# A hybrid decoder step on one core: order of the side work, order of the last head pair, and the memory of the trunk's tiles

## The chip, the cores and the metric

The kernel runs on one core of one Trainium2 chip. The metric is the device time of one launch in microseconds (us); smaller is better. Every number of a profile comes from one profiled execution; the time before is the median of three runs.

## The reference, cut to what matters

One layer of a decoder with 1024 features is computed in float32 for a prompt of 2048 tokens and for 8 sample requests of 4 tokens each (32 sample tokens), which share the weights:

```
a = rmsnorm(h); [qa|fa|ia|ga|qb|kb|vb] = a @ w_in          # 7 groups of 512 columns
h = h + concat(HGRN2(qa,fa,ia,ga), DilatedAttn(qb,kb,vb)) @ w_o
h = h + ConvFFN(rmsnorm(h))                                 # 1024 -> 2816 -> 1024, gate with a 3-tap convolution
h = h + sigmoid(rmsnorm(h) @ w_ple_gate) * (p @ w_ple_proj)
y = rmsnorm(h)
```

HGRN2 is a gated linear recurrence of 4 heads of 128. DilatedAttn has 8 heads of 64; each query reads keys of three dilations (window 128 step 1, window 512 step 4, window 2048 step 16), each dilation has its own softmax statistics, and the three are combined by their maxima and sums. A sample request reads a cache of 2048 keys and values beside its new tokens and a stored recurrent state. Outputs are y for both, the recurrent states, the caches and the convolution's last rows.

## The kernel before, in words

Matmuls that need float32 precision are done as three fast ones: every operand is split into a rounded high part and a low part (on ACT, L913 or L982, and on DVE, L914 or L983), and `mm3` (L136 to L138) adds high x high, high x low and low x high in PSUM.

Four stages follow each other. The input stage multiplies by `w_in` in two token blocks; the recurrence of the prompt (`hgrn_unit`, 8 units) runs beside its second block. Then come the prompt's attention and the sample requests side by side. The last is the trunk: output projection, FFN and embedding, each over three token blocks of 704, 704 and 672 tokens (`TRUNK`, the last with the 32 sample tokens), in the order out 0, 1, 2, FFN 0, 1, 2, embedding 0, 1, 2.

`attn_phase` treats the 8 heads as four pairs p. Per pair there are two kinds of blocks (di = 0: the step-4 residue classes, di = 1: the near window) in four query chunks c of 512 tokens; a unit is one block of 128 queries for both heads, or for one head where a block has over two tiles of keys. This makes 40 units per pair, 160 in all, in the order of the list `units`. A loop over x makes the scores of unit x (L719, L720, then minimum on DVE, L724, and exponential on ACT, L725), transposes the probabilities of unit x - 2 (L732, copied at L734) and multiplies those of unit x - 3 with the values (L744). Keys and queries of a pair lie in four large tiles (qS, q4, kH, kL); the next pair's are loaded into `stage` tiles and laid there during the present pair's last units. When both kinds of a chunk are done, `merge` combines them: statistics go through DRAM (`stats_d`, L650), coefficients too (`coef_d`, L672 and L676, `cf`), POOL multiplies (L681), DVE adds (L683), and the result is stored in row 4 + p of `mix_d` (L684). A merge is spread over the turns 0, 2, 3, 4, 8 and 9 after its last unit.

Beside it runs a generator `others`: the last unit of the prompt's recurrence, the sample's recurrence (`hgrn_sample`), and the sample's attention (`attn_sample`). The last reads 32 tiles `skt` of 1 MB of the cache, adds a mask (`sneg`), takes the exponential, multiplies by how many dilations contain a key (`smult`, L860; `smultn`, L861), transposes (L870), multiplies with the values (L884, L889), and stores into `mix_d` (L897). The loop that drives both makes one turn of the attention, and on two of each five turns one step of `others`, with high priority:

```
    for turn in itertools.count(1):
        if not step(main, 1):
            break
        if turn % 5 in (1, 3):
            first(side, 1)
```

The order on each engine's queue is not the order of the program. A planner simulates the time line, takes instructions by priority (the program's order) as their inputs come ready in its simulation, and gives tiles a place among the free ones of their pool. Each engine then executes its list in order. A pool that is opened with `reuse_waits="tile"` (the helper `pools`) passes its memory on tile by tile; the pools `hsp`, `s_c`, `s_k` and `s_w` of the sample work are opened without it. Pools are laid one after the other from one end of SBUF, those of the recurrence from the other end.

In the trunk, `wide` takes a tile of 704 floats per partition from the pool `tw` (48 of them): raw activations, their high and low parts, residuals h, and working tiles of the FFN. Weights come through `raw` (pool `tr`, 8 tiles), are split into `w` (pool `tp`, 9 tiles of 4 KB), and accumulate in 8 PSUM banks (`tm`). `out_prep` loads the 8 rows of `mix_d` of a block and splits them; `out_block` first multiplies two output tiles m together, row after row (`dense_first`), then the other six. While a block's last products run, the next block's preparation is advanced (`ahead`). `ffn_prep` makes sums and differences of the halves of its 8 rows (L1084 to L1087, split at L982, L983), because the FFN's gate and up products use Strassen's seven products (`strassen`); it holds 28 tiles for the whole FFN block, beside h.

## Time and profile before

| | |
|---|---|
| median of 3 runs | 3115.41 us (3111.81 to 3116.32) |
| profiled execution | 3108.7 us, span 3106.7 us |
| mean granted TensorE clock | 0.980 |
| busy share PE / PEld / DVE / ACT / POOL | 96 / 90 / 72 / 42 / 26% |
| DMA | 468.54 MB, mean 151 GB/s |

PE is TensorE's matmuls, PEld its weight loads, DVE VectorE, ACT ScalarE, POOL GpSimd, SP the queue that issues nearly all loads and stores. The span runs from the first to the last instruction. The granted clock is a share of 2.4 GHz; 0.50 is the lower level, 1.2 GHz. A window's row gives the stretch, its length, the busy time of each engine with the number of instructions, the clock, the busy share of the DMA engines (a figure may round above 1) and GB/s.

### The profile page before, as it was taken

What the parts mean: (1) busy time and instruction counts of PE and PEld (TensorE: products, weight loads), DVE (VectorE), ACT (ScalarE), POOL (GpSimd) and SP (SyncE); (2) the same over time, 40 slices, a digit from 0 to 9 for tenths busy, and PEclk for the clock granted to TensorE, in tenths of its full rate; (3) what the DMA queues carried; (4) which work ended last, traced back from release to release, by engine and by line L of the source; (5) the groups of instructions that cost most, each with busy time, mean ns of one, the idle gap of its engine ahead of it and who ended that gap; (6) DMA issues with size and microseconds to landing.
All of it is one profiled execution on the core that took longest, in us unless ns stands there. A gap on an engine that the chain in (4) does not pass through costs nothing.

```text
span 3106.7 us, 52031 instructions
## 1 busy us (share of the span) xinstructions
PE 2995.4 (96%) x19035; PEld 2781.7 (90%) x19035; DVE 2240.2 (72%) x4670; ACT 1296.8 (42%) x2813; POOL 808.2 (26%) x655
## 2 busy tenths in 40 slices
PE   9999999999889996999999999999999999999998
PEld 8988899987667654998999998999998999999997
DVE  7424667857688874469777779777778877787786
ACT  4111422222366654335444445444444444445443
POOL 1211122222344431003222223322222322232331
PEclk9999999999999997999999999999999999999998
DMA  6334333342536898675434443434433544436453
GB/s 186 98 114 137 105 103 110 103 150 71 152 85 164 251 275 253 212 254 189 163 114 138 136 131 137 167 134 143 137 115 128 185 144 144 137 111 210 141 176 130
DMA packets 265505, 468.54 MB, mean 151 GB/s; under 512 B 39520, under 2 KB 107232, under 8 KB 263456
## 3 DMA queue, kind: packets, MB, share of 16 engines
q1 hardware_dynamic: 261664, 398.22, 40.4%
q10 hardware_dynamic: 3584, 66.98, 6.1%
q8 instruction: 150, 2.46, 0.3%
q14 instruction: 107, 0.88, 0.1%
HBM read 381.60 MB, written 150.48 MB: 171 GB/s over the span
## 4 chain that ended last, share of the span: by engine, by line
PE 52%; DVE 5%; issue 1%; ACT 1%; DMA 1%; SPq 0%; DVEq 0%; ACTq 0%
PE mm L136 17%; PE mm L137 17%; PE mm L138 17%; DVE w L914 1%; DVE w L1171 1%; DVE w L983 0%; PE mm L123 0%; ACT w L982 0%; DVE w L1256 0%; DMA w<-in_pT_dram 0%; DVE w L1084 0%; DVE w L1245 0%; PE mm L108 0%; DMA w<-hn_d 0%; DVE w L1287 0%
## 5 line engine op out<-in xcount | busy, mean ns | idle before, releaser
L137 PE MATMUL mm<-w 128*128 128x352 f32 (+3 forms) x3768 | 1211.2, 322 | 3.2 <-DVE w L983 1.9
L136 PE MATMUL mm<-w 128*128 128x352 f32 (+3 forms) x3768 | 1176.5, 323 | 30.7 <-ACT w L982 10.4
L138 PE MATMUL mm<-w 128*128 128x352 f32 (+3 forms) x3768 | 1204.0, 322 | 0.0
L136 PEld LDWEIGHTS mm<-w 128*128 128x128 f32 x3768 | 705.7, 189 | 38.4 <-ACT w L982 22.0
L137 PEld LDWEIGHTS mm<-w 128*128 128x128 f32 x3768 | 714.3, 190 | 6.8 <-DVE w L983 4.6
L138 PEld LDWEIGHTS mm<-w 128*128 128x128 f32 x3768 | 712.4, 189 | 0.1
L914 DVE TENSOR_TENSOR w<-raw,w 128x512 fp32r<-128x512 f32 x718 | 556.7, 791 | 161.3 <-ACT w L913 155.4
L913 ACT CAST w<-raw 128x512 fp32r<-128x512 f32 x718 | 430.9, 619 | 380.5 <-PE mm L138 251.0
L1171 DVE TENSOR_TENSOR w<-w,mm 128x352 f32<-128x352 f32 (+1 forms) x528 | 257.2, 506 | 89.8 <-PE mm L138 79.9
L1103 POOL TENSOR_TENSOR raw<-raw 128x512 f32<-128x512 f32 x66 | 99.7, 1511 | 739.1 <-DMA raw<-in_w_down_dram 203.4
L1111 POOL TENSOR_TENSOR raw<-raw 128x512 f32<-128x512 f32 x66 | 94.6, 1433 | 398.5 <-DVE w L914 398.5
L725 ACT ACTIVATE P<-P,st 128x256 f32<-128x256 f32 (+3 forms) x256 | 134.6, 528 | 85.2 <-DVE st L724 82.9
L1126 ACT COPY s<-mm 128x352 f32<-128x352 f32 (+1 forms) x198 | 88.1, 445 | 173.4 <-PE mm L138 167.2
L301 PE MATMUL mm<-wh,xh 128*128 128x512 f32 x352 | 142.0, 405 | 0.0
L303 PE MATMUL mm<-wh,xl 128*128 128x512 f32 x352 | 140.9, 401 | 0.0
L302 PE MATMUL mm<-wl,xh 128*128 128x512 f32 x352 | 140.5, 400 | 0.0
L142 POOL TENSOR_SCALAR wh<-wraw 128x512 fp32r<-128x512 f32 x96 | 73.0, 771 | 244.7 <-PE o L137 83.0
L136 PE MATMUL mm<-xh,wh 128*128 128x384 f32 (+2 forms) x384 | 125.1, 330 | 5.8 <-ACT xh L199 5.2
L724 DVE CUSTOM_DVE_ANT_0 P<-S,mask 128x256 f32<-128x256 f32 (+3 forms) x256 | 105.9, 445 | 29.3 <-PE S L720 22.8
L964 POOL TENSOR_TENSOR w<-w 128x704 f32<-128x704 f32 (+2 forms) x42 | 76.3, 1823 | 192.7 <-ACT w L963 191.9
L138 PE MATMUL mm<-xh,wl 128*128 128x384 f32 (+2 forms) x384 | 125.0, 329 | 1.2 <-DVE wl L224 1.2
L224 DVE TENSOR_TENSOR wl<-wraw,wh 128x512 fp32r<-128x512 f32 x104 | 83.0, 817 | 59.0 <-POOL wh L142 53.8
(330 smaller groups left out, 5046.7 us busy)
## 6 DMA issues: line engine op xcount, KB each, us to landing
raw<-in_w_gate_dram SPq DMA_DIRECT2D x132, 256.0 KB
raw<-in_w_up_dram SPq DMA_DIRECT2D x132, 256.0 KB
raw<-in_w_down_dram SPq DMA_DIRECT2D x132, 256.0 KB
out_sk_dram<-in_cache_k_dram ACTq DMA_DIRECT2D x56, 584.0 KB
out_sv_dram<-in_cache_v_dram ACTq DMA_DIRECT2D x56, 584.0 KB
wraw<-in_w_in_dram SPq DMA_DIRECT2D x104, 256.0 KB
w<-h_d SPq DMA_DIRECT2D x48, 352.0 KB
raw<-in_w_ple_gate_dram SPq DMA_DIRECT2D x64, 256.0 KB
```

The lines of the kernel that those rows point to most:

```text
L136: PE.matmul(ps, lhsT=wh, rhs=xh, start=first, stop=False, skip_group_check=read)
L137: PE.matmul(ps, lhsT=wh, rhs=xl, start=False, stop=False, skip_group_check=read)
L138: PE.matmul(ps, lhsT=wl, rhs=xh, start=False, stop=last, skip_group_check=read)
L301: PE.matmul(ps, lhsT=xh[k][:, js], rhs=wh, start=k == 0, stop=False)
L302: PE.matmul(ps, lhsT=xh[k][:, js], rhs=wl, start=False, stop=False)
L303: PE.matmul(ps, lhsT=xl[k][:, js], rhs=wh, start=False, stop=k == NK - 1)
L724: V.tensor_tensor_reduce(pe, s[:, w * i:w * i + w], bl.mask, 1.0, 3e38, ALU.add, ALU.min, mn)
L725: A.activation(pe, pe, AF.Exp, bias=mn, scale=-1.0, accum_out=st[:, bl.r, hh, 0:1])
L913: A.copy(w[:, 0], raw)
L914: V.tensor_sub(w[:, 1], raw, f32(w[:, 0]))
L1103: G.tensor_add(s1, a21, a22)
L1171: V.tensor_add(h[m][:, cs], h[m][:, cs], ps[:, :H])
```

## The change

The side work: the sample's attention runs before the sample's recurrence, both in pools with `reuse_waits="tile"`; `s_k` has three tiles instead of two; a side step follows every second turn. The tables `smult` and `smultn` and their two multiplications are gone: the logarithm of the multiplicity stands in `sneg` and `snegn`, which are added before the exponential. The attention: units of pair 3 are in the order chunk by chunk, both kinds of a chunk after each other; the last addition of its merges is on POOL; `v` has 6 buffers instead of 5, `P` 4 instead of 5. The trunk: its pools are laid in another order, `tw` has 40 tiles, and a new pool `thh` has 8 of the same size (`held`), used for the raw rows in `out_prep`, for h in the FFN and for the high parts in embedding block 1; out block 0 starts with one output tile instead of two.

```diff
@@ -632,7 +632,7 @@
 
         def values_chunk(p, di, c):
 
-            raw = wk.tile([128, 4, 128], F32, name="v", bufs=5)
+            raw = wk.tile([128, 4, 128], F32, name="v", bufs=6)
             cols = v_d[512 * c:512 * c + 512, 128 * p:128 * p + 128]
             if di == 0:
                 SP.dma_start(raw, cols.rearrange("(i r) c -> i r c", r=4))
@@ -680,7 +680,7 @@
             for i in range(2):
                 G.tensor_mul(parts[i], parts[i], cf[:, i])
             yield
-            V.tensor_add(parts[1], parts[1], parts[0])
+            (G if p == 3 else V).tensor_add(parts[1], parts[1], parts[0])
             SP.dma_start(mix_d[:, 4 + p, 512 * c:512 * c + 512], parts[1])
 
         class Block:
@@ -714,7 +714,7 @@
                 bl.st = st
                 w = 128 * bl.nk
                 s = pS.tile([128, 512], F32, name="S")
-                self.pe = wk.tile([128, 512], F32, name="P", bufs=5)
+                self.pe = wk.tile([128, 512], F32, name="P", bufs=4)
                 for i, hh in enumerate(self.heads):
                     PE.matmul(s[:, w * i:w * i + w], lhsT=bl.q(hh), rhs=bl.k(kH, hh), start=True, stop=False)
                     PE.matmul(s[:, w * i:w * i + w], lhsT=bl.q(hh), rhs=bl.k(kL, hh), start=False, stop=True)
@@ -746,12 +746,14 @@
 
         units, begin = [], {}
         for p in range(4):
-            for di in range(2):
-                for c in range(4):
-                    begin[p, di, c] = len(units)
-                    for r in range(4):
-                        bl = Block(p, di, c, r)
-                        units += [Unit(bl, (0, 1))] if bl.nk < 3 else [Unit(bl, (0,)), Unit(bl, (1,))]
+
+            order = [(di, c) for di in range(2) for c in range(4)] if p < 3 else \
+                [(di, c) for c in range(4) for di in range(2)]
+            for di, c in order:
+                begin[p, di, c] = len(units)
+                for r in range(4):
+                    bl = Block(p, di, c, r)
+                    units += [Unit(bl, (0, 1))] if bl.nk < 3 else [Unit(bl, (0,)), Unit(bl, (1,))]
         n = len(units)
         todo, staged = {}, []
 
@@ -812,12 +814,8 @@
 
     def attn_sample(cp, kp, wk, pps):
         NKEY = 1024 + NS
-        mult = cp.tile([128, 1024], F32, name="smult")
-        SP.dma_start(mult, I["s_mult"])
         neg = cp.tile([128, 1024], F32, name="sneg")
         SP.dma_start(neg, I["s_neg"])
-        multn = cp.tile([128, 2, NS], F32, name="smultn")
-        SP.dma_start(multn, I["s_multn"])
         negn = cp.tile([128, 2, NS], F32, name="snegn")
         SP.dma_start(negn, I["s_negn"])
         hmask = cp.tile([128, 512], F32, name="shm")
@@ -857,8 +855,6 @@
             V.tensor_tensor(nm[:, 0:1], nm[:, 0:1], nm[:, 1:2], op=ALU.min)
             V.tensor_tensor(nm[:, 0:1], nm[:, 0:1], nm[:, 2:3], op=ALU.min)
             A.activation(P, P, AF.Exp, bias=nm[:, 0:1], scale=-1.0)
-            V.tensor_mul(P[:, :1024], P[:, :1024], mult)
-            V.tensor_mul(P[:, 1024:], P[:, 1024:], multn[:, g])
             V.reduce_sum(l[:, 0:1], P, axis=mybir.AxisListType.X)
             V.reciprocal(l[:, 1:2], l[:, 0:1])
             yield
@@ -899,7 +895,7 @@
 
 
 
-    def trunk(cst, rp, ev, sm, tw, sh, wp, pmm):
+    def trunk(cst, rp, ev, sm, tw, hp, sh, wp, pmm):
         def raw_tile():
             return rp.tile([128, 512], F32, name="raw")
 
@@ -926,6 +922,9 @@
 
         def wide(T, dt=F32):
             return tw.tile([128, 704], dt, name="w")[:, :T]
+
+        def held(T, dt=F32):
+            return hp.tile([128, 704], dt, name="h")[:, :T]
 
         def dense(parts, xh, xl, ks=range(NK), ends=(0, NK - 1)):
 
@@ -996,7 +995,7 @@
             s.order = (2, 3, 4, 5, 0, 1, 6, 7) if b == 0 else range(NK)
             s.mh, s.ml = {}, {}
             for k in s.order:
-                raw = wide(T)
+                raw = held(T)
                 SP.dma_start(raw, mix_d[:, k, t0:t0 + T])
                 s.mh[k], s.ml[k] = halves(raw, T)
                 yield
@@ -1005,7 +1004,8 @@
             t0, T, _ = TRUNK[b]
             H = T // 2
             chunks = ((0, H), (H, H))
-            first = dense_first([weight(I["w_o"][m]) for m in range(2)], chunks, s.mh, s.ml, s.order)
+            n1 = 2 if b else 1
+            first = dense_first([weight(I["w_o"][m]) for m in range(n1)], chunks, s.mh, s.ml, s.order)
             flush(1)
             ssq = wide(T)
             h = []
@@ -1019,10 +1019,10 @@
             more()
             more()
             for m in range(NK):
-                w = None if m < 2 else weight(I["w_o"][m])
+                w = None if m < n1 else weight(I["w_o"][m])
                 more()
                 hm = h[m]
-                for ps, c0, cn in dense_all(w, chunks, s.mh, s.ml, first[m] if m < 2 else None):
+                for ps, c0, cn in dense_all(w, chunks, s.mh, s.ml, first[m] if m < n1 else None):
                     V.tensor_add(hm[:, c0:c0 + cn], ps[:, :cn], hm[:, c0:c0 + cn])
                 SP.dma_start(h_d[:, m, t0:t0 + T], hm)
                 sum_sq(m, hm, ssq, T)
@@ -1259,7 +1259,7 @@
                     V.tensor_sub(lo, gms[i], f32(hi))
                     parts[i] = hi, lo
                 if f == 0:
-                    h = [wide(T) for _ in range(NK)]
+                    h = [held(T) for _ in range(NK)]
                     for m in range(NK):
                         SP.dma_start(h[m], h_d[:, m, t0:t0 + T])
                 todo.extend(downs(b, f, parts, h))
@@ -1280,7 +1280,7 @@
             s.ssq = wide(T)
             for m in range(NK):
                 hm = raw[m]
-                hi, lo = wide(T, F32R), wide(T, F32R)
+                hi, lo = (held if b == 1 else wide)(T, F32R), wide(T, F32R)
                 g = gains[:, 2, m:m + 1]
                 A.activation(hi, hm, AF.Copy, scale=g)
                 sum_sq(m, hm, s.ssq, T, eng=G)
@@ -1470,17 +1470,17 @@
         for h in range(4):
             SP.dma_start(O["ps"][h], S[h])
         hgrn_st.close()
-        with tc.tile_pool(name="hsp", bufs=1) as hp:
-            yield from hgrn_sample(hp, pps)
-        with tc.tile_pool(name="s_c", bufs=1) as cp, tc.tile_pool(name="s_k", bufs=2) as kp, \
-                tc.tile_pool(name="s_w", bufs=1) as wk:
-            yield from attn_sample(cp, kp, wk, pps)
+        with ExitStack() as st:
+            pool = pools(st)
+            yield from attn_sample(pool("s_c", 1), pool("s_k", 3), pool("s_w", 1), pps)
+        with ExitStack() as st:
+            yield from hgrn_sample(pools(st)("hsp", 1), pps)
 
     side = others()
     for turn in itertools.count(1):
         if not step(main, 1):
             break
-        if turn % 5 in (1, 3):
+        if turn % 2:
             first(side, 1)
     first(side, 1000)
     attn_st.close()
@@ -1497,8 +1497,10 @@
         SP.dma_start(cst["conv_s"], I["conv_s"])
         cst["halo"] = cp.tile([128, NF, 2], F32, name="halo")
         G.memset(cst["halo"], 0.0)
-        trunk(cst, pool("tr", 8), pool("te", 2), pool("ts", 1), pool("tw", 48), pool("th", 6), pool("tp", 9),
-              pool("tm", 8, space=PSUM))
+
+        tr, tp, ts, th, te, tw, hp = [pool(n, k) for n, k in (
+            ("tr", 8), ("tp", 9), ("ts", 1), ("th", 6), ("te", 2), ("tw", 40), ("thh", 8))]
+        trunk(cst, tr, te, ts, tw, hp, th, tp, pool("tm", 8, space=PSUM))
         SP.dma_start(O["pc"], cst["halo"])
         SP.dma_start(O["sc"], cst["conv_s"])
 
@@ -1551,16 +1553,15 @@
     mw = (dist <= 128).astype(f) + ((dist % 4 == 0) & (dist <= 512)).astype(f)
     md = (np.repeat(np.arange(4), 128)[None, :] == t[:, None]).astype(f)
     mult = np.concatenate([mw, md], 1)
-    c["s_mult"] = mult
-    c["s_neg"] = np.where(mult > 0, 0.0, BIG).astype(f)
+    logs = lambda n: np.where(n > 0, -np.log(np.maximum(n, 1.0, dtype=np.float64)), BIG).astype(f)
+    c["s_neg"] = logs(mult)
     mn = np.zeros((128, 2, NS), f)
     for g in range(2):
         for r in range(128):
             b, tt = 4 * g + r // 32, r % 4
             mn[r, g, 4 * b:4 * b + tt] = 1.0
             mn[r, g, 4 * b + tt] = 3.0
-    c["s_multn"] = mn
-    c["s_negn"] = np.where(mn > 0, 0.0, BIG).astype(f)
+    c["s_negn"] = logs(mn)
     head = (np.arange(128) % 32) // 4
     c["s_hmask"] = (head[:, None] == np.arange(512)[None, :] // 64).astype(f)
     bt = (np.arange(128) // 32) * 4 + t
```

## Rows read from the trace of the kernel before

**Rows 1.** The page's table of engines: busy time, share of the span, instructions
```profile
PE 2995.4 (96%) x19035; PEld 2781.7 (90%) x19035; DVE 2240.2 (72%) x4670; ACT 1296.8 (42%) x2813; POOL 808.2 (26%) x655
```

**Rows 2.** Windows: stretch, length, busy us (x) of PE, PEld, DVE, ACT, POOL, clock, DMA
```profile
820.00:1190.00 370.00, 334.06 (x2786) 239.46 (x2785) 302.38 (x980) 236.18 (x681) 158.48 (x135) 0.94 0.70 198
1190.00:1240.00 50.00, 27.60 (x158) 16.65 (x158) 18.48 (x36) 13.03 (x27) 10.35 (x8) 0.63 0.82 255
1240.00:1390.00 150.00, 150.00 (x963) 149.94 (x963) 86.10 (x152) 50.50 (x79) 3.86 (x3) 1.00 0.67 223
```

**Rows 3.** Windows of 10 us around the trunk's start, same columns
```profile
1200.00:1210.00 10.00, 3.00 (x16) 0.36 (x16) 1.03 (x2) 0.59 (x1) 2.78 (x3) 0.63 1.03 309
...
1220.00:1230.00 10.00, 2.73 (x8) 2.39 (x9) 6.31 (x10) 5.46 (x10) 0.00 (x0) 0.50 0.72 218
1230.00:1240.00 10.00, 7.08 (x24) 6.62 (x24) 3.58 (x5) 3.95 (x6) 0.00 (x0) 0.50 0.92 341
```

**Rows 4.** PE in order of time: start us, length us, group, [idle before <- releaser]
```profile
1190.15 0.28 PE L719 MATMUL S<-kH,qS 128*128 128x256 f32 x1
...
1211.34 1.93 PE L884 MATMUL s<-skt,sPT 128*32 128x512 f32 x8 [4.57 <-DMA skt<-in_v_d_dram]
...
1227.27 1.54 PE L136 MATMUL mm<-w 128*128 128x352 f32 x4 [9.38 <-DVE w L914]
...
1234.33 1.54 PE L136 MATMUL mm<-w 128*128 128x352 f32 x4 [2.92 <-ACT w L982]
```

**Rows 5.** ACT in order of time, the first weights of the trunk
```profile
1222.28 4.26 ACT L913 CAST w<-raw 128x512 fp32r<-128x512 f32 x8 [13.99 <-DMA mix_d<-mixs]
```

**Rows 6.** SP in order of time, the sample's store and the load behind it
```profile
1220.12 0.37 SPq L897 DMA_DIRECT2D mix_d<-mixs  x1
1220.83 0.32 SPq L1000 DMA_DIRECT2D w<-mix_d  x1
```

**Rows 7.** Groups of lines, 1190 to 1225 us: xcount, busy us, mean ns, idle before
```profile
L681 POOL TENSOR_TENSOR o<-o,cf 128x512 f32<-128x512 f32 x8 | 10.4, 1318 | 68.3 <-DMA cf<-coef_d 68.3
L884 PE MATMUL s<-skt,sPT 128*32 128x512 f32 x40 | 7.1, 787 | 9.2 <-DMA skt<-in_v_d_dram 9.2
L744 PE MATMUL acc<-pt,v 128*64 128x128 f32 x48 | 3.9, 285 | 0.0
L683 DVE TENSOR_TENSOR o<-o,o 128x512 f32<-128x512 f32 x4 | 3.8, 954 | 14.2 <-POOL o L681 14.1
...
L732 PE MATMUL PT<-c_ident,P 128*128 128x128 f32 x16 | 2.6, 287 | 0.0
...
L889 PE MATMUL s<-v_s,sPTn 32*32 32x512 f32 x8 | 1.9, 1056 | 0.0
L894 PE MATMUL s<-ssel,som 128*128 128x16 f32 x8 | 1.9, 377 | 0.9 <-DVE som L891 0.9
```

**Rows 8.** Groups of lines, 850 to 1750 us: the sample's multiplicities
```profile
L860 DVE TENSOR_TENSOR sP<-sP,smult 128x1024 f32<-128x1024 f32 x2 | 3.8, 1906 | 0.0
...
L861 DVE TENSOR_TENSOR sP<-sP,smultn 128x32 f32<-128x32 f32 x2 | 1.7, 845 | 0.0
```

**Rows 9.** Waits of PE, 770 to 1320 us: total us, times, longest us
```profile
PE s L870 <- DVE sP L860: 1.6, 1, 1.6
```

**Rows 10.** Waits of SP's queue, 780 to 1250 us
```profile
SPq L650 <- DMA stat_d<-st: 6.0, 3, 3.9
```

**Rows 11.** Windows of 77.7 us, in the sample's attention
```profile
1087.80:1165.50 77.70, 74.04 (x607) 45.69 (x609) 54.79 (x177) 45.51 (x134) 24.99 (x22) 0.98 0.90 277
```

**Rows 12.** Groups of lines, 1395 to 1470 us: the FFN's first combinations
```profile
L983 DVE TENSOR_TENSOR w<-w 128x704 fp32r<-128x704 f32 x12 | 13.3, 1144 | 0.1
...
L1084 DVE TENSOR_TENSOR w<-w 128x352 f32<-128x352 f32 x4 | 3.2, 790 | 0.0
...
L1087 DVE TENSOR_TENSOR w<-w 128x352 f32<-128x352 f32 x4 | 2.4, 596 | 0.0
...
L1085 DVE TENSOR_TENSOR w<-w 128x352 f32<-128x352 f32 x4 | 2.1, 516 | 0.0
```

## Prediction

> **What bounds the kernel now.** I read the page's engine table first: PE is busy for 96% of the span [rows 1], so time can only come from stretches in which PE is idle or its clock is low. The windows say where. While the prompt's attention and the sample requests run side by side (820 to 1190 us), PE is busy 334.1 of 370 us at a clock of 0.94. From 1190 to 1240 us it is busy 27.6 of 50 us at 0.63. From 1240 to 1390 us the trunk keeps it busy throughout: 963 matmuls in 150 us, 0.156 us each [rows 2]. The hole at the trunk's start is the largest of the profile. Finer windows show it: 3.00, 2.73 and 7.08 us of work in 10, at a clock of 0.63 and then 0.50, the 1.2 GHz level [rows 3].
>
> PE's timeline names what it waited for. The last scores of the prompt's attention begin at 1190.15 us. Then the sample attention's last value products come, the last one 4.57 us late behind its load. The trunk's first matmul starts at 1227.27 us after 9.38 us of waiting for a split weight, and another group at 1234.33 us after 2.92 us for a split activation [rows 4]. ACT's timeline gives the reason: the first weight split began at 1222.28 us, after 13.99 us idle, released by the sample's store `mix_d<-mixs` [rows 5]; that store was issued at 1220.12 us, and the first load of a mix row stands directly behind it [rows 6]. So the trunk does not wait for data. It waits for memory: its weight tiles lie over the sample's pools, which are opened without `reuse_waits="tile"`, and come free as a whole when the pool's last store is done.
>
> To put the hole in one number: before 1240 us PE ran 8 + 24 = 32 trunk matmuls [rows 3], worth 32 x 0.156 = 5.0 us at full rate. The trunk behaves as if it had started, at full rate, at 1235.0 us.
>
> **The change, part by part.** Signs are for the time; minus is a gain.
>
> *Sides earlier and tile by tile.* A side step on every second turn instead of two of five: the side has about 65 steps (10 for the last recurrence unit, 15 for the sample's, 40 for its attention, from the yields), so it ends near turn 130 of 173, not near 163. Its new pools release single tiles, and `tp` no longer lies over them. The trunk's memory is then bound by the prompt's attention itself. By tile sizes, `tp`'s first two tiles lie over the `stage` tiles, which are done some 38 units before the end: enough for one weight, the `n1 = 1`. The 8 `held` tiles lie beyond the sample's recurrence, so raw mix rows can be loaded ahead. The first hi/lo tiles lie over kH and kL, free at the last scores, and some over the side's area. If the trunk's work followed the last scores directly: 1190.2 - 1235.0 = -44.8.
>
> *What still comes after the last scores.* The last units' transposes (L732, 2.6) and value products (L744, 3.9): +6.5 us [rows 7].
>
> *The sample's work that moves ahead of them.* L884 7.1, L889 1.9, L894 1.9: 10.9 us as run [rows 7]. The part at the 0.50 clock halves when it runs inside the attention. The last of L884's five groups took 1.93 us [rows 4], against 1.42 on average; if the last two, L889 and L894 ran at half clock, 7.7 us become 3.8 and 7.1 remain. I take +8, ends 7 and 10.9.
>
> *No multiplicities.* L860 and L861 go, 3.8 + 1.7 = 5.5 us of DVE [rows 8], and two loads; their logarithm is in the mask that is added anyway. PE waited for them once, 1.6 us [rows 9]. I take -1.6, ends 0 and -5.5.
>
> *Trunk matmuls in the attention's last gaps.* With one weight split early and mix rows held, the two chunks of w_o[0] (48 matmuls, 7.5 us) can run in PSUM banks that the side leaves, between attention units. PE leaves 36 of 370 us idle there [rows 2], about 2 us in the last 20, and gaps open when the last units' chains run out. I take -3, ends 0 and -7.5.
>
> *Last pair by query chunks.* The same 40 units in another order, so no work is added. Merges of chunks 0 and 1 (all that trunk block 0 needs) come some 12 units earlier. New is that a chunk's statistics are read back 4 units after they are written, not 16 or more: SP's queue has waited for such a landing, 3.9 us at the longest [rows 10], and behind it wait the state and weight loads of SP and then PE. Four times 3.9 is 15.6, the far end; four units last 4 x 370/160 = 9 us [rows 2], which covers one such landing, so I take 0. Six `v` tiles are what this order keeps alive. `P` with four buffers costs 0, since scores and transposes are two units apart. If it did bind, each unit would wait for the transposes of the one before, and the 2.6 us that 16 of them took [rows 7] would stand in the open for each 4 units.
>
> *Additions on POOL.* Four additions of 0.95 us on DVE become four of about 1.32 on POOL, by POOL's multiplication in the same place [rows 7]. Nobody waits for them but a store: 0, ends -3.8 and +5.3. Beside it stands a rule of the Trainium skill (SBUF — State Buffer, Who interferes with whom): a VectorE instruction with two SBUF inputs and a GpSimd one that reads SBUF shut each other out, the later one for the other's whole length. By that the four would hold DVE off for up to 5.3 us, and the sum below would be 5 us worse; the rows show L683 at 0.95 beside POOL's work, which does not decide it.
>
> *40 tiles and 8 held, in place of 48.* In the FFN's inner loop nothing changes: 28 combinations and 12 working tiles are 40, and h takes the other 8 as before. Embedding block 1 uses `held` as well. But at the end of out block 2 nothing uses `held`, and the FFN's first combinations are made ahead: 16 halves, 8 h and some 3 more, with 8 raw and 4 split tiles, are 39; each further step wants 4 and gives back 2. Before, all four steps fit into 48; now hardly one does. A step is two differences L1084/L1086 (0.79 and like L1085), L1085 0.52, L1087 0.60 and one L983 of 1.14, some 3.4 us of DVE [rows 12]. Three steps late are 10.2 us if DVE has nothing else to do meanwhile; DVE is full there and has splits to do. I take +4, ends 0 and +10.2.
>
> Sum: -44.8 + 6.5 + 8 - 1.6 - 3 + 4 = -30.9. The profiled execution took 3108.7 us (span 3106.7); the median of the runs is 3115.4, 6.7 above. I apply the difference to the median: 3115.4 - 30.9 = 3084.5, and say 3085. All good ends give -44.8 + 6.5 + 7 - 5.5 - 7.5 = -44.3, 3071; all bad ones -44.8 + 6.5 + 10.9 + 10.2 = -17.2, 3098, and with POOL's 5.3 us on the path 3104.
>
> **Rivals.**
> *(B) A new wait at the same place.* Mix row 7 needs the last pair's merge: five transfers in a row. POOL waited 68.3 us in all for such coefficients while large loads were under way [rows 7]. If PE's order, which the planner sets, puts matmuls of w_o[0] among the last units and the row lands late, PE stands there, attention behind it. From the last scores at 1190.15 [rows 4] to the last store at 1220.12 [rows 6] such a chain had 30 us at most; it now starts 12 units, 12 x 2.3 = 28 us, earlier, so it would be 2 us late, and if half of these units are quicker without the side, 15. Time 3085 + 15 = 3100. Against: POOL's wait was behind the sample's loads, which are gone by then. Beside it the Trainium skill (DMA: Bandwidth & Descriptors, Queues, rings and completion order) says that a DMA engine takes a queue's descriptors in ring order, so small transfers stand behind 1 MB ones; that agrees with the 68.3 us.
> *(C) More.* The attention itself loses idle time, since the sample's loads no longer end it and the last pair runs alone. Of its 36 us [rows 2] a half, 18: 3085 - 18 = 3067. Against: DVE is busy 302 of 370 us there, and its share does not move.
> *(D) It does not do what it says.* The sample attention is bound by DMA (share 0.90 at 277 GB/s [rows 11]), ends as late as before, and its reads still end last: 3115. Against: 32 loads of 1.05 MB take 121 us at that rate, and they may start at turn 20 in place of 62, 42 x 2.3 = 97 us earlier.
> *(E) Slower.* The 40 tiles starve the trunk where one block's halves are made beside another's: four boundaries (out 0/1, out 1/2, out 2/FFN, embedding 0/1), each up to 10.2 us, 40.8 in place of my 4: 3085 + 37 = 3122. It decides above 8.7 us each, where the four eat all of 34.9. Against: three of the four have their raw or hi tiles in `held`.
>
> **Numbers.** (A) 0.59, (B) 0.16, (C) 0.10, (D) 0.07, (E) 0.08. A measurement of this kernel can't tell less than 0.2%, 6.2 us. Faster are A, B and C, 0.85; same is D, 0.07; slower is E, 0.08. The range for 8 in 10 takes A's 3071 to 3098, most of B and half of C: 3066 to 3105.
>
> **What would show it.** Right: no PE idle over 3 us between the last scores and the trunk's full rate; the first weight split before the last scores; the sample attention's last products before 1130 us; clock 1.0 in the windows after. Slot shortage: PE's idle time after out block 2 grows by some 4 us, with most of L1084 to L1087 after the block's last matmul. Wrong would be: the trunk's first matmul more than 15 us after the last scores; the last scores themselves later than 1205 us; or idle time at every boundary of the trunk.

## The result, and the profile after

The changed kernel takes 3097.88 us (median of 6 runs, 3093.52 to 3102.19) against 3115.51 of the kernel before (6 runs, 3111.81 to 3123.39): ratio 0.9941, 95% interval 0.9927 to 0.9956, 17.6 us less. The forecast was 30.9 us less. The profiled execution took 3096.28 us, its span is 3094.5 us, the clock 0.981.

The windows of [rows 2] and [rows 3], with the same columns, now read:

```profile
820.00:1190.00 370.00, 328.52 (x2781) 233.62 (x2780) 291.70 (x944) 231.25 (x665) 164.47 (x143) 0.94 0.75 214
1190.00:1240.00 50.00, 42.69 (x288) 36.97 (x287) 32.03 (x80) 22.99 (x53) 8.34 (x6) 0.86 0.76 252
1240.00:1390.00 150.00, 150.00 (x963) 149.94 (x963) 92.28 (x158) 51.48 (x82) 5.77 (x4) 1.00 0.72 246
```

```profile
1200.00:1210.00 10.00, 5.30 (x41) 3.11 (x40) 10.00 (x24) 7.07 (x19) 4.54 (x3) 0.70 0.79 243
1210.00:1220.00 10.00, 8.86 (x35) 7.92 (x36) 5.54 (x10) 4.34 (x7) 1.13 (x1) 0.62 0.45 135
1220.00:1230.00 10.00, 8.53 (x52) 8.00 (x51) 2.66 (x3) 2.60 (x4) 2.67 (x3) 1.00 0.64 215
1230.00:1240.00 10.00, 10.00 (x65) 10.00 (x64) 5.74 (x10) 3.24 (x5) 0.00 (x0) 1.00 1.04 400
```

The hole of 1190 to 1240 us holds 42.69 us of PE work where it held 27.60. But from 1200 to 1210 us DVE is full, 10.00 of 10, and PE has 5.30. PE in order of time names what it waits for there (to be read against [rows 4]):

```profile
1197.69 0.28 PE L720 MATMUL S<-kL,qS 128*128 128x256 f32 x1
...
1201.81 0.44 PE L732 MATMUL PT<-c_ident,P 128*128 128x128 f32 x2 [0.84 <-ACT P L725]
...
1203.53 1.18 PE L732 MATMUL PT<-c_ident,P 128*128 128x128 f32 x4 [0.69 <-ACT P L725]
...
1206.53 1.12 PE L744 MATMUL acc<-pt,v 128*64 128x128 f32 x8 [0.76 <-ACT pt L734]
1210.12 0.47 PE L584 MATMUL s<-c_ident,hso 128*128 128x128 f32 x1 [2.46 <-DVE hso L582]
1210.52 0.37 PE L669 MATMUL PT<-c_ident,w 128*16 128x128 f32 x1
1211.92 0.96 PE L136 MATMUL mm<-w 128*128 128x352 f32 x2 [1.02 <-ACT w L981]
...
1222.26 0.42 PE L136 MATMUL mm<-w 128*128 128x352 f32 x1 [0.61 <-ACT w L981]
...
1223.55 0.43 PE L137 MATMUL mm<-w 128*128 128x352 f32 x1 [0.87 <-DVE w L982]
```

The last score starts at 1197.69 us, the trunk's first matmul at 1211.92. No trunk matmul runs ahead of the attention's and the recurrence's last steps. DVE in order of time, and POOL beside it, show what keeps L582:

```profile
1202.76 0.68 DVE L910 TENSOR_TENSOR w<-raw,w 128x512 fp32r<-128x512 f32 x1
1203.37 0.68 DVE L734 COPY pt<-PT 128x512 f32<-128x512 f32 x1
1203.97 3.02 DVE L910 TENSOR_TENSOR w<-raw,w 128x512 fp32r<-128x512 f32 x2
1206.91 1.22 DVE L97 TENSOR_TENSOR rs_t<-rs_y 128x1 f32<-128x1 f32 x1
1208.05 1.28 DVE L910 TENSOR_TENSOR w<-raw,w 128x512 fp32r<-128x512 f32 x2
1209.25 0.16 DVE L663 TENSOR_TENSOR wl<-w,in 128x8 f32<-128x8 f32 x1
...
1209.71 0.35 DVE L582 TENSOR_SCALAR hso<-s,rs_y 128x128 f32<-128x128 f32 x1
```

```profile
1203.48 2.95 POOL L681 TENSOR_TENSOR o<-o,cf 128x512 f32<-128x512 f32 x2 [17.26 <-DMA raw<-in_w_o_dram]
1206.51 1.60 POOL L683 TENSOR_TENSOR o<-o,o 128x512 f32<-128x512 f32 x1
```

L910 is the split of a weight (L914 before). Nine splits run between 1199.38 and 1209.3 us, ahead of the small steps of the last merge (L663 to L666) and of the recurrence's scaling (L582), on which L669 and L584 depend, and these stand ahead of the trunk in PE's order. ACT is crowded in the same way: DVE has the last minimum (L724) ready at 1198.78 us, and the last exponential (L725), which needs it, starts 4.6 us later, with six casts of weights (L909, 3.3 us) in between. The first of these casts begins 24 us earlier than in [rows 5], and block 0's eight mix rows (`h<-mix_d`, L999) are loaded from 1131.87 us on, the last at 1176.29, not from 1220.83 [rows 6]:

```profile
1198.07 0.62 ACT L909 CAST w<-raw 128x512 fp32r<-128x512 f32 x1
...
1199.09 2.17 ACT L909 CAST w<-raw 128x512 fp32r<-128x512 f32 x4
...
1201.66 1.13 ACT L909 CAST w<-raw 128x512 fp32r<-128x512 f32 x2
...
1203.38 0.50 ACT L725 ACTIVATE P<-P,st 128x256 f32<-128x256 f32 x1
...
1221.43 1.46 ACT L981 CAST w<-h 128x704 fp32r<-128x704 f32 x2 [6.15 <-POOL o L681]
```

```profile
1176.29 0.38 SPq L999 DMA_DIRECT2D h<-mix_d  x1
```

The last line of ACT explains PE's two short waits behind 1220 us: the casts of block 0's last two mix rows wait 6.15 us for POOL's multiplication in the last merge. Their rows were loaded long before, so it is probably the memory of their tiles that this multiplication gives back; no run tested it.

For comparisons I use one number, the gap G: from the start of the last score to the point from which the trunk would have run at full rate (start of its 101st recorded matmul less 100 x 0.159 us, the spacing of its matmuls at the full clock in the kernel before). Of the kernel before G is 45.0 us (1190.3 to 1235.3), of the changed one 19.2 (1197.7 to 1216.9); the forecast was 6.5 - 3 = 3.5.

### The profile page after: what moved, and what is told of

The parts are those of the page before. It is cut to its first block, busy times and chain, and to the rows that moved or that the text cites. A ratio compares the mean times of both kernels' runs of the same rounds, so it can differ in the third digit from the quotient of the medians.

```text
span 3094.5 us, 52057 instructions
## 1 busy us (share of the span) xinstructions
PE 2992.3 (97%) x19035; PEld 2785.2 (90%) x19035; DVE 2233.4 (72%) x4662; ACT 1295.2 (42%) x2813; POOL 806.6 (26%) x659
## 3 DMA queue, kind: packets, MB, share of 16 engines
q8 instruction: 150, 2.46, 0.3%
## 4 chain that ended last, share of the span: by engine, by line
PE 80%; DVE 12%; DMA 3%; issue 2%; ACT 1%; POOL 1%; SPq 0%; DVEq 0%; ACTq 0%; POOLq 0%
PE mm L136 18%; PE mm L137 18%; PE mm L138 18%; PE mm L301 3%; PE mm L302 3%; PE mm L303 3%; PE acc L744 1%; PE lv L441 1%; PE PT L732 1%; DVE w L910 1%; DVE P L724 1%; PE lv L301 1%; PE lv L303 1%; PE lv L302 1%; PE S L719 1%
## 5 line engine op out<-in xcount | busy, mean ns | idle before, releaser
L137 PE MATMUL mm<-w 128*128 128x352 f32 (+3 forms) x3768 | 1212.4, 322 | 4.3 <-DVE w L982 4.3
L138 PE MATMUL mm<-w 128*128 128x352 f32 (+3 forms) x3640 | 1164.0, 322 | 0.0
L136 PE MATMUL mm<-w 128*128 128x352 f32 (+3 forms) x3640 | 1138.7, 323 | 18.2 <-ACT w L981 8.7
L137 PEld LDWEIGHTS mm<-w 128*128 128x128 f32 x3768 | 712.9, 189 | 8.0 <-DVE w L982 7.8
L136 PEld LDWEIGHTS mm<-w 128*128 128x128 f32 x3640 | 681.8, 189 | 24.6 <-ACT w L981 10.6
L910 DVE TENSOR_TENSOR w<-raw,w 128x512 fp32r<-128x512 f32 x718 | 563.1, 799 | 179.5 <-ACT w L909 172.7
L138 PEld LDWEIGHTS mm<-w 128*128 128x128 f32 x3640 | 687.7, 189 | 0.1
L909 ACT CAST w<-raw 128x512 fp32r<-128x512 f32 x718 | 431.9, 620 | 396.3 <-PE mm L138 277.2
L1171 DVE TENSOR_TENSOR h<-h,mm 128x352 f32<-128x352 f32 (+1 forms) x528 | 257.6, 506 | 83.8 <-PE mm L138 83.2
L725 ACT ACTIVATE P<-P,st 128x256 f32<-128x256 f32 (+3 forms) x256 | 134.3, 527 | 75.5 <-DVE st L724 68.4
L724 DVE CUSTOM_DVE_ANT_0 P<-S,mask 128x256 f32<-128x256 f32 (+3 forms) x256 | 105.6, 445 | 29.7 <-PE S L720 25.3
```

The source lines that it names most:

```text
L136: PE.matmul(ps, lhsT=wh, rhs=xh, start=first, stop=False, skip_group_check=read)
L137: PE.matmul(ps, lhsT=wh, rhs=xl, start=False, stop=False, skip_group_check=read)
L138: PE.matmul(ps, lhsT=wl, rhs=xh, start=False, stop=last, skip_group_check=read)
L724: V.tensor_tensor_reduce(pe, s[:, w * i:w * i + w], bl.mask, 1.0, 3e38, ALU.add, ALU.min, mn)
L725: A.activation(pe, pe, AF.Exp, bias=mn, scale=-1.0, accum_out=st[:, bl.r, hh, 0:1])
L909: A.copy(w[:, 0], raw)
```

## The experiments

Each kernel was timed beside the kernel before; ratios are to that. All are edits of the changed kernel but one. Two questions lead: what fills G, and which part of the change closes the old hole.

### Without the sample's recurrence

```diff
         with ExitStack() as st:
-            yield from hgrn_sample(pools(st)("hsp", 1), pps)
+            z = pools(st)("hsp", 1).tile([128, 4, 128], F32, name="hsz")
...
```

> The changed kernel without the arithmetic and the loads of the sample's recurrence; its two outputs are filled with zeros. G is the time from the last scores of the prompt's attention to the trunk's start, reckoned back from its full rate: 19.2 us in the changed kernel (1197.6 to 1216.8), 44.8 before. Theory T1 (the last step of the sample's recurrence, L584, stands in PE's queue ahead of the trunk and waits for DVE): G falls to about 7 us, and with the recurrence's own PE work gone the time is about 3098 - 12 - 8 = 3078. T2 (weight splits, nine of them now free to run in the attention's tail, fill ACT and DVE, and the last merge's transpose L669, which also stands ahead of the trunk, waits behind them): G stays at 14 us or more, the time is 3098 - 8 - 3 = 3087. T3 (the attention's own last units and the low clock): G stays at 17 or more, 3090.

Measured: 3084.05 us, ratio 0.9903 (0.9875 to 0.9931). Zeros are stored for the recurrence's outputs. The side ends long before the last scores, which start at 1188.4 us, 9.3 earlier; G is 18.5. So the gap isn't the recurrence's: what its absence saves is its own work. Nor is it the late end of the side, which the prediction had near turn 130 of 173.

### The recurrence's last chain moved into the trunk

```diff
-        PE.transpose(pt[:, 0], o, ident)
...
+        late.append(sample_out)
```

> The changed kernel with the recurrence's last chain (square, root, transpose, store) moved behind the first output tile of out block 0; only a copy out of PSUM stays. T1: L584 is gone from before the trunk, G falls from 19.2 by 6 to 10 us, the time to about 3090. T2: L669 still waits behind the splits, G falls by 0 to 3 us, 3096. T3: no change, 3098.

Measured: 3119.49 us, ratio 1.0024 (1.0010 to 1.0037). Without L584 the merge's transpose stands first in PE's order and waits as long (L663 here, 2.92 us against 2.46); and the moved chain stops the trunk a second time (L989 is its transpose, L987 the DVE step before it):

```profile
1212.13 0.37 PE L663 MATMUL PT<-c_ident,w 128*16 128x128 f32 x1 [2.92 <-DVE w L660]
1213.52 0.96 PE L138 MATMUL mm<-w 128*128 128x352 f32 x2 [1.02 <-ACT w L975]
...
1235.48 0.47 PE L989 MATMUL mm<-c_ident,w 128*128 128x128 f32 x1 [6.86 <-DVE w L987]
```

The first wait is DVE's backlog (9.85 of 10 us busy from 1200 to 1210), not the step that stands in line for it. The second is a new one: L987 stands on DVE behind an addition that waits 4.78 us for a load of x:

```profile
1234.71 0.52 DVE L1035 TENSOR_TENSOR w<-mm,w 128x352 f32<-128x352 f32 x1 [4.78 <-DMA w<-in_xT_dram]
```

G is 30.9.

### Weights of output tiles 1 to 7 split later

```diff
...
+                if b == 0 and m >= n1:
+                    with tc.issue_after(made[5].ins):
+                        w = weight(I["w_o"][m])
...
```

`made[5]` is the high part of the sixth mix row; the other branch of the condition is as before.

> The changed kernel with the weights of output tiles 1 to 7 of out block 0 split behind the sixth activation row, so two splits and not nine stand in the attention's tail. T2: L669 and the recurrence's root are no longer held on DVE and ACT, G falls by 6 to 10 us, the time to about 3090. T1: the recurrence's chain is as long as it was, G falls by 0 to 3. T3: no change.

Measured: 3086.97 us, ratio 0.9918 (0.9895 to 0.9942). L669 comes 6.8 us behind the last score (1192.19), not 12.8, and the trunk's first matmul 9.0, not 14.2 (L983 is here the row's split that was L981):

```profile
1195.97 0.66 PE L744 MATMUL acc<-pt,v 128*64 128x128 f32 x8 [0.28 <-DVE pt L734]
...
1199.00 0.27 PE L669 MATMUL PT<-c_ident,w 128*16 128x128 f32 x1 [1.19 <-DVE w L666]
...
1201.21 0.59 PE L136 MATMUL mm<-w 128*128 128x352 f32 x2 [1.10 <-ACT w L983]
```

G is 12.9, 6.3 less: the splits' share. The last scores also come 5.5 us earlier than in the changed kernel (1192.2 against 1197.7 us), and the sample's attention, which no split of the trunk's weights stands beside, ends 5.2 us earlier (1131.6 against 1136.8); so this part is not the splits': with the same edit and 41 tiles (below) the last scores are at 1197.4 again.

### Both together

The two edits above in one kernel.

> Both of the above at once. T1 and T2 each being half of the cause: G falls by 8 to 12 us, to about 8, the time to 3087. If either alone is the cause, the time is that of the better of the two. T3: 3098.

Measured: 3120.71 us, ratio 1.0023 (1.0011 to 1.0036). The first trunk matmul now comes 8.0 us behind the last score, where with the moved chain alone it came 13.8 behind. But the moved chain's transpose waits 10.91 us: its steps on DVE stand behind a weight split that waits 5.06 us for its cast and an addition that waits 2.69 us for a load of x. G is 30.7, as with the moved chain alone.

### Later splits, and no recurrence

The first and the third edit together.

> The changed kernel with the later splits of the run before and without the sample's recurrence: its loads and arithmetic are left out and zeros are stored for its outputs. It shows the floor of the gap behind the last scores when neither the side nor the splits crowd DVE and ACT. If these two were all that the prediction lacked, the gap falls to 3.5 to 7 us, from 12.9 with the later splits alone and 18.5 without the recurrence alone: 3071 to 3076. If the last units' own chain (softmax, transposes, value products, merge, one behind the other at half clock) makes up the rest, it stays at 11 to 13 us, and only the recurrence's own 13 us on PE go: 3073 to 3078 by the earlier last scores. The gap in the trace decides.

Measured: 3077.28 us, ratio 0.9881 (0.9862 to 0.9899), G 12.5. Neither the side nor seven of the nine splits stand in the way any more, and the gap doesn't fall below 12: the second theory of the expectation holds. From the last score at 1185.73 to the first trunk matmul at 1194.62 lie 8.9 us, of which PE works 6.1 (L732 2.2, L744 3.3) and idles 2.8, one step of the chain after the other:

```profile
1190.89 1.09 PE L744 MATMUL acc<-pt,v 128*64 128x128 f32 x16 [0.47 <-DVE pt L734]
1193.32 0.27 PE L669 MATMUL PT<-c_ident,w 128*16 128x128 f32 x1 [1.34 <-DVE w L666]
1194.62 0.59 PE L136 MATMUL mm<-w 128*128 128x352 f32 x2 [1.02 <-ACT w L983]
```

Then 3.6 us go in the trunk's first matmuls, in part at the lower clock (0.83 from 1190 to 1200 us), in part (1.3) in waits for split mix rows.

### A side step on every turn

```diff
-        if turn % 2:
-            first(side, 1)
+        first(side, 1)
```

> The changed kernel with one edit: a side step on every turn of the attention in place of every second. The prediction let the side end at turn 130 because it counted steps per turn. If the turns set the pace (the prediction's reading), the sample attention, 942 to 1134 us in the changed kernel, takes about half of its 192 us, the side ends some 90 us before the last scores, and the gap between the last scores and the trunk's full rate falls from 19 us towards the 3.5 us that the prediction had: some 3085 us. If the transfers set the pace (32 loads of 1.05 MB at some 200 GB/s are 168 us), the sample attention still takes 170 to 190 us, the side ends where it ends now, and the time stays within 4 us of 3098; instructions that wait longer in the queues may make the last scores a few us later.

Measured: 3101.02 us, ratio 0.9957 (0.9944 to 0.9970), G 19.6. Twice the steps, and the sample attention lasts as long: 934.8 to 1137.2 us, against 933.7 to 1136.8 in the changed kernel and 1015.9 to 1219.8 before (first to last instruction of its lines on the engines). Windows of this kernel:

```profile
940.00:1040.00 100.00, 94.71 (x827) 62.32 (x825) 76.24 (x255) 67.26 (x200) 37.32 (x30) 0.98 0.97 281
1040.00:1140.00 100.00, 86.58 (x785) 57.36 (x786) 71.23 (x231) 61.27 (x177) 47.22 (x39) 0.98 0.90 264
```

So the rate of turns, on which the prediction built, does not set its pace. The DMA share of 0.90 to 0.97 points to the transfers. No run varied them alone, and the tiles of `s_k` may share in it: in the changed kernel two of the longest waits of SP's queue, 11.4 and 8.3 us in all, are loads that wait for matmuls to give a tile back, and with the attention last in the order it takes 188.6 us with three tiles (next run) and 203.9 in the kernel before with two.

### The sample's recurrence first again

```diff
         with ExitStack() as st:
+            yield from hgrn_sample(pools(st)("hsp", 1), pps)
+        with ExitStack() as st:
             pool = pools(st)
             yield from attn_sample(pool("s_c", 1), pool("s_k", 3), pool("s_w", 1), pps)
-        with ExitStack() as st:
-            yield from hgrn_sample(pools(st)("hsp", 1), pps)
```

> The changed kernel with one edit: the sample's recurrence ahead of its attention again, the pools tile by tile and the held tiles kept. In the changed kernel the sample attention takes 203 us and the recurrence behind it 75 us, at whatever rate the turns step them, so either order ends near 1211 to 1219 us. If the order matters (the recurrence at the end leaves the transfers and the trunk's tiles free, the attention at the end does not), the last value products come behind their loads near 1215 us as in the kernel before, the trunk's first matmul is 5 to 15 us later than 1212, and the time is 3104 to 3114. If the order doesn't matter, because only the place of the trunk's tiles counts, it is 3098 within 4.

Measured: 3104.45 us, ratio 0.9969 (0.9956 to 0.9981), G 36.2. The attention ends last again, and its value products wait for loads and for DVE:

```profile
1203.12 1.06 PE L880 MATMUL s<-skt,sPT 128*32 128x512 f32 x8 [2.58 <-DMA skt<-in_v_d_dram]
...
1211.77 1.89 PE L890 MATMUL s<-ssel,som 128*128 128x16 f32 x8 [6.06 <-DVE som L887]
...
1214.90 0.95 PE L136 MATMUL mm<-w 128*128 128x352 f32 x2 [1.03 <-ACT w L981]
```

The last scores come early, at 1189.4 us, but the trunk starts no earlier than 1214.90. Order is worth 0.0028, 8.7 us, by the two ratios.

### 48 trunk tiles in one pool, none held

```diff
-            return hp.tile([128, 704], dt, name="h")[:, :T]
+            return wide(T, dt)
...
-            ("tr", 8), ("tp", 9), ("ts", 1), ("th", 6), ("te", 2), ("tw", 40), ("thh", 8))]
+            ("tr", 8), ("tp", 9), ("ts", 1), ("th", 6), ("te", 2), ("tw", 48), ("thh", 1))]
```

> The changed kernel with one edit: 48 tiles of the trunk in one pool again, none held apart. The prediction took 4 us as the price of the 40 at the end of out block 2 (measured 2 to 3.4) and nothing at the other boundaries. If so, the trunk loses nothing behind out block 2 here, and the time falls by 3 us, to 3095. But the mix rows of block 0 and the 8 h tiles then lie where the pool's turn puts them: if the place of the held tiles (free before the last scores) is what lets rows come early, the first trunk matmul is later than 1212 us and the time rises by 5 to 15 us, 3103 to 3113.

Measured: 3118.55 us, ratio 1.0011 (1.0000 to 1.0021), G 32.6: the whole gain is gone. SP and PE of this kernel:

```profile
1225.84 0.34 SPq L684 DMA_DIRECT2D mix_d<-o  x1
1226.27 4.27 SPq L999 DMA_DIRECT2D w<-mix_d  x8
```

```profile
1230.52 0.95 PE L136 MATMUL mm<-w 128*128 128x352 f32 x2 [17.47 <-ACT w L981]
```

Without the held tiles all eight mix rows are loaded behind the last merge's store, and PE waits 17.47 us for the first. Whether their memory or their place in SP's queue keeps them was not told apart. On the other side, the trunk loses nothing behind out block 2 (its 1210th matmul stands to the kernel before as its 900th did, within 0.1 us). The two profiles' spans differ by 21.8 us; 15.9 of these are there by the trunk's 9000th matmul, the rest arises at the end of the embedding, where other kernels vary too (below).

### The last pair in the old order

```diff
-            order = [(di, c) for di in range(2) for c in range(4)] if p < 3 else \
-                [(di, c) for c in range(4) for di in range(2)]
+            order = [(di, c) for di in range(2) for c in range(4)]
```

> The changed kernel with one edit: the last pair of heads in the order of the other three pairs (dilation, then query chunk). The prediction priced the reorder at nothing by itself, with the merges of chunks 0 and 1, which block 0 of the trunk needs, 12 units (28 us) earlier. If the last merges stand between the last scores and the trunk only as DVE and PE work (splits crowd them), the old order leaves four merges in the last 20 units instead of two, and the gap grows by 3 to 10 us: 3101 to 3108. If the mix rows' landing decides, the trunk starts up to 20 us later, 3118. If the reorder brings nothing, 3098 within 3.

Measured: 3109.59 us, ratio 0.9984 (0.9975 to 0.9993), G 26.3. On POOL three merges begin after 1218 us, in the changed kernel one. The eighth mix row is loaded at 1225.76 us, in the changed kernel at 1176.29, and PE waits for its split (L980):

```profile
1218.33 3.93 POOL L681 TENSOR_TENSOR o<-o,cf 128x512 f32<-128x512 f32 x2 [7.91 <-DMA cf<-coef_d]
1222.33 1.29 POOL L683 TENSOR_TENSOR o<-o,o 128x512 f32<-128x512 f32 x1
1223.94 3.15 POOL L681 TENSOR_TENSOR o<-o,cf 128x512 f32<-128x512 f32 x2 [0.32 <-DMA cf<-coef_d]
```

```profile
1232.14 0.66 PE L136 MATMUL mm<-w 128*128 128x352 f32 x1 [4.71 <-ACT w L980]
```

The reorder that the prediction priced at nothing is worth 0.0043, 13 us.

### The kernel before with tile-by-tile release alone

```diff
-        with tc.tile_pool(name="hsp", bufs=1) as hp:
-            yield from hgrn_sample(hp, pps)
...
+        with ExitStack() as st:
+            yield from hgrn_sample(pools(st)("hsp", 1), pps)
...
```

> The kernel before with one edit: the sample's pools release single tiles, as the prompt attention's do; order of the sides, rate and trunk pools stay. The prediction named the release of the whole pool after the store of 1220 us as the cause of the hole at the trunk's start. If that release is the cause by itself, the first weight split comes before 1210 us in place of 1222, and most of the 17 us appear here: 3100 us. If the cause is the order (the sample attention, which loads over the tiles that the trunk gets, ends last), the trunk's tiles come free only some 5 us earlier and the time is 3108 to 3116.

Measured: 3114.32 us, ratio 1.0003 (0.9992 to 1.0013), G 43.2. Nothing moves; ACT waits 14.00 us for the same store as in [rows 5]:

```profile
1221.27 4.25 ACT L913 CAST w<-raw 128x512 fp32r<-128x512 f32 x8 [14.00 <-DMA mix_d<-mixs]
```

It isn't the release as a whole that kept the trunk's tiles: with single tiles released, the first cast still waits for the attention's last store, so its tile lies over memory that the sample attention uses to its end.

### Later splits, and the last pair's addition on DVE

The edit of the later splits, and:

```diff
-            (G if p == 3 else V).tensor_add(parts[1], parts[1], parts[0])
+            V.tensor_add(parts[1], parts[1], parts[0])
```

> The later splits, and the last pair's addition back on DVE. The prediction priced the move to POOL at nothing (ends -3.8 and +5.3). If that holds, 3087 within 3, as with the later splits alone. If POOL's addition, longer than DVE's and on the way from the last merge to the mix rows, holds block 0's second chunk or the splits beside it, the time falls by 2 to 5 us; if DVE is the engine that is short in the last 20 us, it rises by 1 to 4.

Measured: 3102.64 us, ratio 0.9964 (0.9952 to 0.9977), G 21.7. DVE and PE:

```profile
1213.78 0.69 DVE L683 TENSOR_TENSOR o<-o,o 128x512 f32<-128x512 f32 x1 [8.41 <-POOL o L681]
1214.39 4.89 DVE L984 TENSOR_TENSOR w<-h,w 128x704 fp32r<-128x704 f32 x6
```

```profile
1215.33 0.66 PE L137 MATMUL mm<-w 128*128 128x352 f32 x1 [9.25 <-DVE w L984]
```

On DVE the addition waits 8.41 us for POOL's multiplication, and six mix rows' splits stand behind it. On POOL it stands behind the multiplication anyway. Against the later splits alone (ratio 0.9918, G 12.9) the move back costs 8.8 us of G, and the two intervals don't meet. Without the later splits the move was not tested.

### Later splits, and 41 tiles

The edit of the later splits, and:

```diff
-            ... ("tw", 40), ("thh", 8))]
+            ... ("tw", 41), ("thh", 8))]
```

> The later splits, and 41 tiles in the trunk's pool in place of 40 (one more is what fits beside the 8 held). Behind out block 2 the changed kernel loses 2 to 3.4 us against the kernel before, and the later splits lose 4.2 to 4.8; with 48 tiles nothing was lost there. If single tiles are what is missing, one more gives back a quarter to a half of it: 3085. If several are missing at once, the loss behind out block 2 stays within 1 us: 3087.

Measured: 3096.20 us, ratio 0.9941 (0.9927 to 0.9956); the profiled execution has G 12.1 and a span of 3084.6 us, but the other five runs lie at 3095 to 3099. The loss behind out block 2 (from the trunk's 900th to its 1210th matmul, against the kernel before) is 4.0 us, where it is 4.8 with the later splits alone: one tile gives 0.8 back. The ratio equals the changed kernel's. So that the later splits shorten the gap is shown by three profiles (12.9, 12.5, 12.1 against 19.2, 18.5, 19.6), where nothing else comes to stand in it (with the moved chain it stays at 30.7, with the addition on DVE it is 21.7). That a kernel with them is faster is not shown: the interval of the later splits alone reaches from 0.9895 to 0.9942, and 0.9941 was measured here. What the gap is in the five slower runs is not known.

## Why the prediction was right or wrong

The direction, the hole and the bound on PE were right; 17.6 us of 30.9 came. At the trunk's start the prediction had a gain of 34.9 us (44.8 - 3.5 - 6.4) before the 4 us for the tiles, and the profiles show 18.4 (45.0 - 19.2 - 7.4). By steps:

- *What still comes after the last scores*: this step failed. It counted PE's work there, 6.5, and took 3 off for trunk matmuls in the gaps, as if the trunk followed at once at full rate: 3.5. Measured is 19.2. In the changed kernel's 14.2 us from the last score to the first trunk matmul, PE works 8.4 us (L732 and L744 alone 7.3, slower for the lower clock) and idles 5.8; the trunk's first matmuls lose another 5.0, in part at half clock (0.62 from 1210 to 1220 us), in part (1.5) in waits for split mix rows; and no trunk matmul ran in a gap. The runs split the 15.7 us of error: 6.3 by weight splits that the change itself sets free, in front of the last merge on DVE and ACT (6.0 in the pair without the recurrence, 18.5 against 12.5); the other 9.4 remain with the splits out of the way (9.0 with the recurrence left out as well), as the last units' own chain and the trunk's slow first matmuls, by the trace; no run took these apart. The prediction's own sign of being right, no idle time of PE over 3 us, held (the longest is 2.46): the gap is made of many short waits and a low clock. The prediction asked only whether the splits could come early, not what DVE, which has the last chain's small steps, would then put off.
- *The sample's work ahead of the last scores*, +8 - 1.6: the last scores moved from 1190.3 to 1197.7, 7.4, against 6.4. Right in kind, but that it agrees within 1 us is luck: kernels with the same work ahead have them at 1192.2 (later splits), 1197.4 (41 tiles) and 1200.9 (a step on every turn). What the multiplicities alone bring was not measured.
- *The hole's cause*: half right. Memory held the trunk, but not because pools came free as a whole (release alone: 1.0003). It takes the sample's order, the held tiles and the pair's order together: taking back one alone costs 8.7, 21.8 and 13 us by the ratios, in all more than the 17.6 that all of them bring. These gains don't add: whichever is missing, something of its own ends last (the sample's value products, the first mix row, the eighth mix row). The third tile of `s_k`, the buffers of `v` and `P`, the one output tile at the start and the multiplicities were not taken back one by one.
- *The side ends near turn 130, the sample attention before 1130 us*: wrong. The attention's lines end at 1136.8 and the recurrence at 1210.9, and twice the steps end them no earlier. So rival D's mechanism (the attention's pace is the transfers', not the turns') is borne out as far as it was tested, and its effect wasn't: what ends last in the new order is the recurrence, and the run without it shows that this fills no gap.
- *Additions on POOL at 0*: a gain, not 0, in the kernel with the later splits: there DVE would wait 8.41 us in front of the rows' splits. The Trainium skill's rule (SBUF — State Buffer, Who interferes with whom) does show in the trace: two L910 took 3.02 us beside L681, where one alone takes 0.68, and L97 took 1.22 beside L683; some 1.7 and 1.1 us more. Only the second is the moved addition's, since L681 was on POOL before too, and it is well under the 8.41 that the move avoids.
- *40 tiles*, +4: the trunk loses 3.3 us from its 900th to its 1210th matmul, 2.0 to its 1400th, and 0.1 to the 1210th with 48 tiles. The mechanism is right at this place, but most of it comes back: the lead over the kernel before is 17.7 us at the 900th matmul and 17.3 at the 9000th, so over the trunk +4 was too much. The rows of a step add up to 3.6 us, not the 3.4 of the prediction; its far end would be 10.7. Rival E falls, since the boundaries between out blocks lose under 1 us.
- *Last pair by chunks at 0*: mis-sized in isolation, 13 us; the sum had that gain inside the -44.8.
- *Rivals B and C*: B's time, 3100, came close, but not its mechanism: the eighth mix row is loaded at 1176.29 us, and from its first matmul to 1390 us the trunk waits at most 0.87 us. A wait for mix rows appears when the held tiles or the pair's order are taken back (17.47 and 4.71 us). C did not come: PE's idle time from 820 to 1190 us is 41 us, not less than the 36 of before.
- *The range*: that 3097.9 lies inside it is in part luck. The far end of its sum, 3098, was made of the sample's work, the multiplicities, the tiles and the matmuls in the gaps. Only the last of these came out at its far end; the 6.5 us behind the last scores, the term that failed, had no far end at all.

One difference between the two profiles isn't the change's. At the end of embedding block 1 the trunk loses 4.9 us against the kernel before (12.4 us lead at the end, after 18.4 at the trunk's 101st matmul and 17.3 in the third FFN block). But the kernel before with tile release alone, whose trunk is unchanged, loses 5.0 us at the same place: there PE waits for DVE's L114,

```profile
3021.06 2.93 PE L123 MATMUL mm<-c_ident,rs_y 128*128 128x128 f32 x12 [4.72 <-DVE rs_v L114]
```

and the clock falls (0.74 from 3010 to 3030 us). In the profiled execution of the kernel before the same wait was 3.08 us and the clock stayed at 1.00 there; it did without the loss, and lay 6.8 us under its median; so the medians' 17.6 is the better measure, not the spans' 12.2.

## What to carry to other kernels

When a change closes a hole between two stages, write the last unit's whole chain across all engines into the sum, not only its work on the busiest engine, and ask what the newly freed work of the next stage will do on the engines of that chain. Where several conditions gate one start, price the change as a whole: here the one part taken alone brought nothing, and each of three parts left out lost half of the gain or more. An instruction that waits for another engine can be better placed on that engine's queue, even where it runs nearly twice as long there (here 1.27 against 0.69 us): in front of other work it would hold up its own.

## What was not expected of the hardware

The sample attention takes 200 to 207 us in all kernels here but one, at any of three rates of steps (188.6 us in the kernel with the recurrence first and three tiles): 33.6 MB in 203 us are 165 GB/s, not the 200 that one expectation took, while all queues together move 264 to 281. Two-input instructions of DVE and POOL that lie beside each other take turns: two L910 (0.64 each in pairs elsewhere) and two L681 (1.26 each at 1218.87 us) together end 3.5 us after the first starts, near the sum of 3.8 and far over the 2.5 of the longer pair.
